# Layer norms taken row by row between the products of a macaron encoder layer

## The chip, the core and the metric

The kernel runs on one core of a Trainium2 chip. The time is the device time of one execution in microseconds (us). The core has five engines, each with its own queue of instructions that it works off in order: TensorE (PE) multiplies matrices, VectorE (DVE) and ScalarE (ACT) do arithmetic on rows, GpSimd (POOL) does some of it too and issues a few transfers, and SyncE (SP) issues nearly all transfers (DMAs) between device memory and the on-chip memory SBUF. Engines wait for each other by semaphores.

## The reference

One encoder layer, run on two inputs, of 512 and 1024 rows of 1024 values, with the same weights:

```
x = layer_norm(ALPHA * x + 0.5 * swiglu(x, ffn1_wg, ffn1_wu, ffn1_wd), ln_g[0], ln_b[0])
x = layer_norm(ALPHA * x + hybrid_mixer(x, ...),                       ln_g[1], ln_b[1])
x = layer_norm(ALPHA * x + 0.5 * swiglu(x, ffn2_wg, ffn2_wu, ffn2_wd), ln_g[2], ln_b[2])

def swiglu(x, wg, wu, wd):            # wg, wu: 1024 x 2816, wd: 2816 x 1024
    return (silu(x @ wg) * (x @ wu)) @ wd

def layer_norm(x, g, b):
    mu = mean(x); xc = x - mu; var = mean(xc * xc)
    return xc * rsqrt(var + 1e-5) * g + b
```

The mixer projects the rows to a gated recurrence, an attention and a Fourier part and joins them by an output projection. All is float32.

## The kernel before

The 1536 rows of both inputs form 12 tiles of 128 rows, a "row" from here on. `ffn` is called twice, as ffn1 ahead of the mixer and as ffn2 behind it. Each call handles the 12 rows in two halves of six: an early phase (`ffn1a`, half 0) and a late phase (`ffn1b`, half 1). A phase goes over 11 pairs (`NP`) of 256 hidden columns. Each pair has 14 "up" products, seven for each of the two blocks of hidden columns, because the matrices are multiplied by a scheme with seven products in the place of eight; a product is 12 matmuls of 128x384 (`up<-xt,…`). Every number is held as the sum of two fp32r pieces, a high and a low one: `split` makes them by a cast on ACT (L132) and a difference on DVE (L133), and `mm3` (L138) multiplies pieces three ways. From the products DVE and ACT form the hidden values `h`, and the "down" products of a pair (`big<-a,h`, `big<-w,h`) run between the up products of the next; DVE adds them to the six accumulators in SBUF (tile `x`, L456 and L509). In the early phase the prepared weights are written to device memory (`left`), and in the late phase `kept` reads them again (`w<-left`), two loads of 1 MB ahead, each for two products; only pair 0 of the late phase makes its pieces anew (`up<-xt,a`).

The layer norm of half 0 does not stand at the end of the early phase. It is a generator, `norm`, which is advanced from within the products of pair 0 of the late phase (by `between`), in two batches of three rows, by `layer_norm` (L210 to L240). A batch goes through these steps for its rows together: a mean on DVE (L222), a Square with a running sum on ACT (L225), the variance on DVE (L227), its power -0.5 on POOL (L228), and for each row a centre step on DVE (L231: subtract the mean, multiply by the gain). The final step scales by the power and adds the bias. For rows of odd number this is one DVE operation (L238). For rows of even number (`POOLED`) it is an Identity on ACT (L235) and an add on POOL (L236). Then SP stores each row (L240), and afterwards the next six rows are loaded into the freed slots (L160).

The norm of half 1 is at the end of the late phase: the accumulators are finished by the last down products (`down`, L447 to L456) in the row order `last` = 3, 0, 1, 2, 4, 5, and each row's norm follows as a batch of one. For ffn1 this overlaps with the entrance of the mixer: `columns` transposes rows of x1 on PE (`big<-ident,x`, L153), which come from device memory by `load_rows` (L160), and `project` multiplies them by the input weights (`big<-xt,w`). For ffn2 it is the end of the program.

The order on each engine is made by a scheduler from the order in which the code issues work and from priorities; within one engine nothing overtakes afterwards. Tiles live in pools of a few slots by name (`x` has six, `a` five), and an instruction that writes a tile waits until its slot is free.

Of the kernel before, what the change touches and what calls it, by code (L numbers as in the profile page):

```python
# [65 lines left out]
STAGE = 2  # L66
PREP = 3
STREAM = 2
DOWN_AT = (0, 1, 3, 4, 6, 8, 9, 11)
SCRATCH = 2048  # L70
SQ_SCALE = 2.0 ** 64
# [31 lines left out]
class Kernel:  # L103
# [106 lines left out]
    def layer_norm(self, rows, sums, params, dst=None, part=range(TPC)):  # L210

        nc = self.nc
        for t0 in part[::BATCH]:
            ts = range(t0, min(t0 + BATCH, part.stop))
            n = len(ts)
            st = self.tiny("st", [3, TPC])[:, :, :n]
            mean, var, rs = (st[:, i] for i in range(3))
            if sums.shape[2] > 1:
                nc.vector.tensor_reduce(mean, sums[:, t0:t0 + n], axis=mybir.AxisListType.X, op=ALU.add)
                nc.vector.tensor_scalar(mean, mean, -1.0 / D, None, op0=ALU.mult)  # L220
            else:
                nc.vector.tensor_scalar(mean, sums[:, t0:t0 + n, 0], -1.0 / D, None, op0=ALU.mult)  # L222
            for t in ts:
                k = t - t0
                nc.scalar.activation(self.slot("a", [D], BF16), rows[t], AF.Square, bias=mean[:, k:k + 1],  # L225
                                     accum_out=var[:, k:k + 1])
            nc.vector.tensor_scalar(var, var, 1.0 / D, EPS / ALPHA ** 2, op0=ALU.mult, op1=ALU.add)  # L227
            nc.gpsimd.tensor_tensor(rs, var, self.mhalf[:, :n], op=ALU.pow)  # L228
            for t in ts:
                a, k = rows[t], t - t0  # L230
                nc.vector.scalar_tensor_tensor(a, a, mean[:, k:k + 1], params[0], op0=ALU.add, op1=ALU.mult)  # L231
            for t in ts:
                a, k = rows[t], t - t0
                if POOLED(t):
                    nc.scalar.activation(a, a, AF.Identity, scale=rs[:, k:k + 1])  # L235
                    nc.gpsimd.tensor_add(a, a, params[1])  # L236
                else:
                    nc.vector.scalar_tensor_tensor(a, a, rs[:, k:k + 1], params[1], op0=ALU.mult, op1=ALU.add)  # L238
                if dst is not None:
                    STORE(nc, t).dma_start(dst[t], a)  # L240

# [79 lines left out]
    def ffn(self, n, which, src, dst, scr, wscr, first=False, beside=iter(()), staged=iter(()), meanwhile=iter(())):  # L321
# [72 lines left out]
        def up(m, w, got, between, result, fifth=quarter):  # L394
# [33 lines left out]
            out(m, got, 1, 0, a, result)  # L428
            yield

        def out(m, got, i, j, x, result):

            if m == 0:
# [75 lines left out]
                    nc.vector.scalar_tensor_tensor(x, ps, scale, x, op0=ALU.mult, op1=ALU.add)  # L509
                yield  # L510

        def norm(half, accs, parts):
            params = self.ln_params(which, "p")
            for part in parts:
                self.layer_norm(accs, sums[:, half] if half else sums[:, half, :, :1], params, dst[half * HALF:(half + 1) * HALF], part)
                yield

        def prepared(todo, keep):

# [12 lines left out]
        def kept(todo):  # L532
# [3 lines left out]
            def ahead(n=STREAM):  # L536
                while todo and len(slots) < n:
                    w = self.slot("w", [2, 2, h, P], F32R)
                    nc.sync.dma_start(f32(w), f32(todo.pop(0)))
                    slots.append(w)  # L540

            def get():
# [21 lines left out]
            raws = load(0)  # L564
            operand = self.operands_from(scr[0])
        both = lambda w, got, result: chain.from_iterable(zip(*(up(m, w, got, between, result) for m in range(2))))
        last = (3, 0, 1, 2, 4, 5)

        half, tiles = 0, []
        staging = self.operands_to(self.pairs(src[HALF:]), scr[1], [(k, r) for r in range(3) for k in SEVEN])  # L570
# [33 lines left out]
            run(tile() for tile in tiles)  # L604

        half, staging = 1, staged
        norms = norm(0, accs, [range(0, 3), range(3, 6)])
        get, ahead = kept([wscr[p][:, c:c + 2] for p in range(1, NP) for c in range(0, 2 * len(SEVEN), 2)])

        def between():  # L610
            if p == 0:
                next(norms, None)
            if STAGE <= p:
                next(staging, None)

        with self.phase(f"ffn{n}b", LATE_SLOTS, LATE_BANKS):
            steps = iter(())
            for p in range(NP):
                got = {}
                result = "a" if p == NP - 1 else None  # L620
                if p:
                    fifth = lambda: self.slot("d", [HT])
                    products = chain(*(up(m, get, got, between, result, fifth) for m in range(2)))
                else:
                    products = both(first_pair(raws, [[self.slot(t, [h, P]) for t in "bd"] for _ in raws]), got, result)
                for i, _ in enumerate(products):
                    if i in DOWN_AT:
                        next(steps, None)
                    if i == 8:
                        if p < NP - 1:  # L630
                            raw = load_both(p)
# [10 lines left out]
                    steps = down_seven(got, raw)  # L642
            run(staging)
            run(beside)
            norms = norm(1, accs, [range(t, t + 1) for t in last])
            for t in last:
                next(meanwhile, None)
                down(got, ws, t, True)
                next(norms)
            run(meanwhile)  # L650


    def project(self, xts):
# [488 lines left out]
    def run(self):  # L1142
        tc, nc, ins = self.tc, self.nc, self.ins
        with ExitStack() as ctx:
# [153 lines left out]
```

## Time and profile before

| | |
|---|---|
| median of 3 runs | 2902.63 us (2901.74 to 2905.0) |
| the profiled execution's own time | 2902.0 us |
| its span (first to last instruction) | 2899.9 us |
| mean granted TensorE clock | 0.976 of full speed |
| busy share of the span | PE 95%, DVE 67%, ACT 40%, POOL 5% |
| instructions | 39216 |

The busy shares are means over the whole span; what an edit touches is read from the stretch in which it lies. Timelines give the start of a run of like instructions, its length, and in brackets how long the engine had been idle ahead of it and who ended that. Matmuls are pipelined, so a busy PE is not PE at its peak; a lower granted clock shows as longer matmuls.

### The profile page before, as it was taken

Reading aid. Unit: us, or ns where it says so; the run is one execution under the profiler, and the core shown is the slowest. Engines: PE = TensorE matmul, PEld = TensorE weight load, DVE = VectorE, ACT = ScalarE, POOL = GpSimd, SP = SyncE. Lnnn points to the kernel's source line nnn. Section 1 sums busy time; section 2 is a strip of 40 time slices with the busy share of each in tenths; the row PEclk is TensorE's granted clock in tenths of the full one; section 3 lists DMA queues with packets and bytes.
Section 4 is the critical chain, followed back from the end, with each engine's and each line's share of the span. In section 5 each row is a group of like instructions: output and inputs, shape, how many; then the busy total and the mean of one; then the engine's idle time right before and its main releaser. Section 6 shows DMA issues by size and latency. Waiting matters only on the chain. (4 is left out here: it accounts for less than half of the span.)

```text
span 2899.9 us, 39216 instructions
## 1 busy us (share of the span) xinstructions
PE 2762.1 (95%) x14940; PEld 2521.3 (87%) x14940; DVE 1929.5 (67%) x3217; ACT 1157.9 (40%) x2093; POOL 135.1 (5%) x106
## 2 busy tenths in 40 slices
PE   8999999899999989999889986899999998999997
PEld 7999999799999978978678976799999998999996
DVE  7677666677676672453477754667766667676776
ACT  5344334333332344662365642344443334323223
POOL 2000000100000020000000011100000001000002
PEclk9999999999999999999899998899999999999999
DMA  7799766878555572244585486988876586555552
GB/s 255 267 317 317 281 239 227 302 282 271 198 183 193 183 241 83 96 159 141 171 235 153 136 277 216 339 291 303 296 280 242 211 310 221 201 187 191 190 186 104
DMA packets 318076, 650.48 MB, mean 224 GB/s; under 512 B 22976, under 2 KB 194624, under 8 KB 297408
## 3 DMA queue, kind: packets, MB, share of 16 engines
q1 hardware_dynamic: 313888, 641.16, 64.0%
q0 software_dynamic: 4000, 6.82, 0.9%
q8 instruction: 117, 1.92, 0.3%
q14 instruction: 71, 0.58, 0.1%
HBM read 403.06 MB, written 244.84 MB: 223 GB/s over the span
## 5 line engine op out<-in xcount | busy, mean ns | idle before, releaser
L138 PE MATMUL up<-xt,a 128*128 128x384 f32 x4032 | 746.8, 340 | 36.9 <-ACT a L132 27.3
L138 PEld LDWEIGHTS up<-xt,a 128*128 128x128 f32 x4032 | 710.8, 190 | 52.5 <-ACT a L132 31.8
L138 PE MATMUL up<-xt,w 128*128 128x384 f32 x3360 | 617.9, 337 | 0.0
L138 PEld LDWEIGHTS up<-xt,w 128*128 128x128 f32 x3360 | 588.6, 188 | 22.3 <-ACT t L422 10.0
L138 PE MATMUL big<-w,h 128*128 128x512 f32 x1584 | 387.1, 393 | 0.5 <-ACT h L132 0.2
L509 DVE SCALAR_TENSOR_TENSOR x<-big,x 128x512 f32<-128x512 f32 x420 | 277.7, 685 | 111.7 <-PE big L138 109.0
L138 PEld LDWEIGHTS big<-w,h 128*128 128x128 f32 x1584 | 295.3, 188 | 58.7 <-ACT h L132 1.6
L138 PE MATMUL big<-a,h 128*128 128x512 f32 x1260 | 317.9, 394 | 0.0
L138 PEld LDWEIGHTS big<-a,h 128*128 128x128 f32 x1260 | 234.0, 188 | 40.7
L138 PE MATMUL big<-xt,w 128*128 128x512 f32 x1008 | 234.3, 392 | 0.0
L456 DVE SCALAR_TENSOR_TENSOR x<-big,x 128x1024 f32<-128x1024 f32 (+1 forms) x156 | 177.2, 1138 | 81.0 <-PE big L138 78.5
L138 PEld LDWEIGHTS big<-xt,w 128*128 128x128 f32 x1008 | 189.7, 189 | 40.2 <-ACT x L961 0.4
L133 DVE TENSOR_TENSOR a<-w,a 128x512 fp32r<-128x512 f32 x244 | 166.2, 698 | 50.2 <-ACT a L132 48.4
L132 ACT CAST a<-w 128x512 fp32r<-128x512 f32 x244 | 147.6, 621 | 22.3 <-DMA w<-in_ffn_wg 14.0
L132 ACT CAST a<-b 128x512 fp32r<-128x512 f32 x168 | 103.8, 620 | 122.0 <-PE up L138 50.5
L133 DVE TENSOR_TENSOR a<-b,a 128x512 fp32r<-128x512 f32 x168 | 114.9, 688 | 42.9 <-ACT a L132 40.5
L132 ACT CAST h<-t 128x384 fp32r<-128x384 f32 x168 | 86.2, 513 | 119.5 <-DVE t L439 72.3
L138 PE MATMUL mm<-w,xt 128*128 128x256 f32 x960 | 122.4, 285 | 1.3 <-DVE x L1136 1.3
L138 PEld LDWEIGHTS mm<-w,xt 128*128 128x128 f32 x960 | 118.2, 193 | 2.0 <-DVE x L1136 1.9
L403 DVE TENSOR_TENSOR t<-t,up 128x384 f32<-128x384 f32 x88 | 48.7, 553 | 91.7 <-ACT t L402 91.3
L422 ACT COPY t<-up 128x384 f32<-128x384 f32 x88 | 42.2, 479 | 166.6 <-PE up L138 166.4
L414 ACT COPY t<-up 128x384 f32<-128x384 f32 x88 | 42.2, 479 | 161.8 <-PE up L138 161.8
(309 smaller groups left out, 3129.8 us busy)
## 6 DMA issues: line engine op xcount, KB each, us to landing
left<-a SPq DMA_DIRECT2D x280, 512.0 KB, 4.2
w<-left SPq DMA_DIRECT2D x140, 1024.0 KB, 4.7
ops<-a SPq DMA_DIRECT2D x63, 512.0 KB, 4.2
x<-x SPq DMA_DIRECT2D x52, 512.0 KB, 4.3
w<-in_ffn_wg SPq DMA_DIRECT2D x24, 1024.0 KB, 5.8
w<-in_ffn_wu SPq DMA_DIRECT2D x24, 1024.0 KB, 7.4
d<-in_ffn_wd SPq DMA_DIRECT2D x88, 256.0 KB, 4.5
w<-in_ffn_wd SPq DMA_DIRECT2D x20, 1024.0 KB, 5.0
```

The source lines that it names most:

```text
L132: self.nc.scalar.copy(hi, src)
L133: self.nc.vector.tensor_sub(lo, src, f32(hi))
L138: self.nc.tensor.matmul(out, lhs(l), rhs(r), start=first and n == 0, stop=last and n == 2, skip_group_check=onto)
L403: nc.vector.tensor_add(s, s, b)
L414: nc.scalar.copy(s, a)
L422: nc.scalar.copy(s2 := quarter(), a)
L456: nc.vector.scalar_tensor_tensor(accs[t][:, at], pd, scale, accs[t][:, at], op0=ALU.mult, op1=ALU.add, **acc)
L509: nc.vector.scalar_tensor_tensor(x, ps, scale, x, op0=ALU.mult, op1=ALU.add)
```

## The change

A new `layer_norm_row` handles one row: mean, Square, variance and power as before, the centre step on DVE, and the final step always on DVE; the Identity on ACT and the add on POOL are gone. It is a generator with three stages, and `norm` interleaves the stages of neighbouring rows. In pair 0 of the late phase it is advanced once behind each product. The order of rows is now 3, 4, 5, 0, 1, 2 at both places.

In the last pair the second block of products runs in another order (`up_late`, 1 2 3 4 5 0 6), so that the part of the hidden values that rows 3 to 5 need is complete one product before the end; `ending` starts the last down products and the norms after product 12. The weight loads of that pair, whose products are no longer neighbours in `left`, are split in two loads of 512 KB where needed.

Last, `ffn` returns its accumulators, and the mixer's columns for the second and third chunk of four rows are made from the rows in SBUF. Only rows 4 and 5 (half 0) are still loaded from device memory, into slots named `a`. Before, all eight were loaded into slots named `x`.

```diff
+LATE_ORDER = (1, 2, 3, 4, 5, 0, 6)
+    def layer_norm_row(self, a, sums, params, dst):
+        st = self.tiny("st", [3, TPC])
+        mean, var, rs = (st[:, i, :1] for i in range(3))
+        if sums.shape[1] > 1:
+            nc.vector.tensor_reduce(mean, sums, axis=mybir.AxisListType.X, op=ALU.add)
+            sums = mean
+        nc.vector.tensor_scalar(mean, sums, -1.0 / D, None, op0=ALU.mult)
+        nc.scalar.activation(self.slot("a", [D], BF16), a, AF.Square, bias=mean, accum_out=var)
+        yield
+        nc.vector.tensor_scalar(var, var, 1.0 / D, EPS / ALPHA ** 2, op0=ALU.mult, op1=ALU.add)
+        nc.gpsimd.tensor_tensor(rs, var, self.mhalf[:, :1], op=ALU.pow)
+        nc.vector.scalar_tensor_tensor(a, a, mean, params[0], op0=ALU.add, op1=ALU.mult)
+        yield
+        nc.vector.scalar_tensor_tensor(a, a, rs, params[1], op0=ALU.mult, op1=ALU.add)
+        nc.sync.dma_start(dst, a)
+        yield
...
-        def norm(half, accs, parts):
+        def norm(half, accs, rows):
             params = self.ln_params(which, "p")
-            for part in parts:
-                self.layer_norm(accs, sums[:, half] if half else sums[:, half, :, :1], params, dst[half * HALF:(half + 1) * HALF], part)
-                yield
+            late = iter(())
+            for t in rows:
+                row = self.layer_norm_row(accs[t], sums[:, half, t, :2 if half else 1], params, dst[half * HALF + t])
+                next(row)
+                next(late, None)
+                yield
+                next(row)
+                late = row
+                yield
+            next(late, None)
+            yield
...
-                    nc.sync.dma_start(f32(w), f32(todo.pop(0)))
+                    src, (x, y) = todo.pop(0)
+                    if y == x + 1:
+                        nc.sync.dma_start(f32(w), f32(src[:, x:y + 1]))
+                    else:
+                        for i, at in enumerate((x, y)):
+                            nc.sync.dma_start(f32(w)[:, i], f32(src[:, at]))
...
-        last = (3, 0, 1, 2, 4, 5)
+        last = (3, 4, 5, 0, 1, 2)
-        norms = norm(0, accs, [range(0, 3), range(3, 6)])
+        norms = norm(0, accs, last)
...
         def between():
-            if p == 0:
-                next(norms, None)
             if STAGE <= p:
                 next(staging, None)
+        def ending(got, ws):
+            norms = norm(1, accs, last)
+            for t in last:
+                down(got, ws, t, True)
+                next(norms)
+                next(norms)
+                next(meanwhile, None)
+                yield
+            run(norms)
...
-                    products = chain(*(up(m, get, got, between, result, fifth) for m in range(2)))
+                    forms = (up, up) if p < NP - 1 else (up, up_late)
+                    products = chain(*(form(m, get, got, between, result, fifth) for m, form in enumerate(forms)))
                 for i, _ in enumerate(products):
+                    if p == 0:
+                        next(norms, None)
                     if i in DOWN_AT:
                         next(steps, None)
+                    if p == NP - 1 and i == 12:
+                        run(steps)
+                        rest = ending(got, ws)
+                        next(rest)
...
-            xts = [self.columns_from(cols)] + [self.columns(lambda c=c: self.load_rows(chunk(x1, c), "x")) for c in range(1, NCH)]
+            held = []
+            xts = [self.columns_from(cols), self.columns(lambda: self.load_rows(x1[TPC:HALF], "a") + held[:2 * TPC - HALF]),
+                   self.columns(lambda: held[2 * TPC - HALF:])]
...
-            self.ffn(1, 0, xs, x1, scr[0], wscr, True, tables(), self.columns_to(chunk(x1, 0), cols), begun())
+            held += self.ffn(1, 0, xs, x1, scr[0], wscr, True, tables(), self.columns_to(chunk(x1, 0), cols), begun())
```

ACT in pair 0 of ffn1's late phase, before. L225 is the norm's Square, L235 its Identity for even rows, L132 the casts of weight pieces (`a<-b`, `a<-d`), and L402 to L414 copies of products.

```order
L225 ACTIVATE a,st<-x,st 128x1024 x2
L409 COPY t<-up 128x384
L225 ACTIVATE a,st<-x,st 128x1024
L132 CAST a<-b 128x512
L235 ACTIVATE x<-x,st 128x1024 x2
L409 COPY t<-up 128x384
L225 ACTIVATE a,st<-x,st 128x1024 x3
L132 CAST a<-b 128x512
L235 ACTIVATE x<-x,st 128x1024
L414 COPY t<-up 128x384
```

The same place after; L252 is the Square, L133 the casts, L422 and L429 the copies.

```order
L252 ACTIVATE a,st<-x,st 128x1024
L133 CAST a<-b 128x512
L133 CAST a<-d 128x512
L422 COPY t<-up 128x384
L252 ACTIVATE a,st<-x,st 128x1024
L489 ACTIVATE t<-t 128x384
L133 CAST a<-d 128x512
L422 COPY t<-up 128x384
L133 CAST a<-b 128x512
L429 COPY t<-up 128x384
L252 ACTIVATE a,st<-x,st 128x1024
```

The Squares of a batch stood together, and the Identities behind them; now one Square stands every three or four operations, and no Identity.

DVE in the same stretch, before: L227 is the variance, L231 the centre step, L238 the final step, L133 the low pieces (`a<-b,a`).

```order
L231 SCALAR_TENSOR_TENSOR x<-x,st,p 128x1024 x2
L227 TENSOR_SCALAR st<-st 128x3
L231 SCALAR_TENSOR_TENSOR x<-x,st,p 128x1024
L238 SCALAR_TENSOR_TENSOR x<-x,st,p 128x1024
L133 TENSOR_TENSOR a<-b,a 128x512
L231 SCALAR_TENSOR_TENSOR x<-x,st,p 128x1024 x2
L227 TENSOR_SCALAR st<-st 128x3
L231 SCALAR_TENSOR_TENSOR x<-x,st,p 128x1024
L238 SCALAR_TENSOR_TENSOR x<-x,st,p 128x1024 x2
```

After: L254 variance, L256 centre step, L258 final step, L134 the low pieces, L396 and L423 sums of weights and of products.

```order
L254 TENSOR_SCALAR st<-st 128x1
L256 SCALAR_TENSOR_TENSOR x<-x,st,p 128x1024
L134 TENSOR_TENSOR a<-b,a 128x512
L134 TENSOR_TENSOR a<-d,a 128x512
L258 SCALAR_TENSOR_TENSOR x<-x,st,p 128x1024
L423 TENSOR_TENSOR t<-t,up 128x384
L396 TENSOR_TENSOR b<-w,d 128x512
L254 TENSOR_SCALAR st<-st 128x1
L256 SCALAR_TENSOR_TENSOR x<-x,st,p 128x1024
L423 TENSOR_TENSOR t<-t,up 128x384
L134 TENSOR_TENSOR a<-d,a 128x512
```

Nine passes over whole rows stood with one low piece between them; now two to four other operations stand between one row's centre and final step, and there are twelve passes in all.

SP at the end of ffn1, before: L240 stores rows of x1 (`x_9` is row 3 of the late half, `x_6` its row 0), L160 loads rows of x1 for the mixer's columns, L144 and L792 load weights.

```order
L240 DMA x_9_129<-x 128x1024
L144 DMA a<-in_w_in 128x8x128
L160 DMA x<-x_4_124 128x1024
L144 DMA a<-in_w_in 128x8x128
L240 DMA x_6_126<-x 128x1024
L160 DMA x<-x_5_125 128x1024
L240 DMA x_7_127<-x 128x1024
L144 DMA r<-in_w_in 128x8x128
L240 DMA x_8_128<-x 128x1024
L160 DMA x<-x_6_126 128x1024
L240 DMA x_10_130<-x 128x1024
```

After, from the third of the stores on: L259 stores rows, L161 loads them, L145 loads weights, L762 stores columns of the mixer.

```order
L259 DMA x_11_131<-x 128x1024
L145 DMA a<-in_w_in 128x8x128
L145 DMA r<-in_w_in 128x8x128
L259 DMA x_6_126<-x 128x1024
L145 DMA r<-in_w_in 128x8x128
L259 DMA x_7_127<-x 128x1024
L762 DMA rx_76<-d 128x512
L161 DMA a<-x_4_124 128x1024
L161 DMA a<-x_5_125 128x1024
L259 DMA x_8_128<-x 128x1024
```

The loads of `x_4` and `x_5` stood behind one and two of the stores, and now stand behind five; the loads of the six other rows are gone.

## Rows read from the trace of the kernel before

**Rows 1.** Stretches: length, busy PE, PEld, DVE, ACT, POOL, granted clock, DMA.

```profile
546.76:589.12 42.36, 33.33 (x170) 31.39 (x168) 33.99 (x43) 22.65 (x40) 13.43 (x7) 0.84 0.66 248
1062.50:1076.14 13.64, 5.65 (x34) 5.05 (x33) 13.02 (x12) 7.12 (x9) 7.95 (x4) 0.75 0.73 240
2867.81:2899.90 32.09, 15.85 (x70) 12.77 (x69) 25.19 (x54) 11.09 (x16) 15.68 (x9) 0.78 0.25 98
```

**Rows 2.** Waits of PE, whole run: total us, times, longest us.

```profile
PE up L138 <- ACT a L132: 27.3, 8, 6.2
```

**Rows 3.** Timeline of PE, ffn1: start us, us, operation, [idle before, releaser].

```profile
546.76 19.07 PE L138 MATMUL up<-xt,a 128*128 128x384 f32 x108
568.40 1.01 PE L138 MATMUL up<-xt,a 128*128 128x384 f32 x2 [2.57 <-ACT a L132]
574.53 1.91 PE L138 MATMUL up<-xt,a 128*128 128x384 f32 x4 [5.12 <-ACT a L132]
577.78 11.50 PE L138 MATMUL up<-xt,a 128*128 128x384 f32 x54 [1.34 <-DVE a L133]
589.12 6.92 PE L138 MATMUL up<-xt,w 128*128 128x384 f32 x39
...
599.54 1.78 PE L138 MATMUL big<-a,h 128*128 128x512 f32 x7
```

**Rows 4.** Timeline of ACT, the same stretch of ffn1.

```profile
561.88 2.19 ACT L235 ACTIVATE x<-x,st 128x1024 f32<-128x1024 f32 x2 [1.66 <-POOL st L228]
...
572.45 1.15 ACT L235 ACTIVATE x<-x,st 128x1024 f32<-128x1024 f32 x1 [4.09 <-POOL st L228]
```

**Rows 5.** Timeline of DVE, the same stretch of ffn1.

```profile
565.61 4.79 DVE L231 SCALAR_TENSOR_TENSOR x<-x,st,p 128x1024 f32<-128x1024 f32 x2 [1.84 <-ACT a L225]
570.32 0.15 DVE L227 TENSOR_SCALAR st<-st 128x3 f32<-128x3 f32 x1
...
572.45 4.67 DVE L238 SCALAR_TENSOR_TENSOR x<-x,st,p 128x1024 f32<-128x1024 f32 x2 [0.78 <-POOL st L228]
...
577.65 1.28 DVE L133 TENSOR_TENSOR a<-d,a 128x512 fp32r<-128x512 f32 x2
```

**Rows 6.** Timeline of POOL, the same stretch of ffn1.

```profile
563.12 6.19 POOL L236 TENSOR_TENSOR x<-x,p 128x1024 f32<-128x1024 f32 x2 [1.27 <-ACT x L235]
```

**Rows 7.** Timeline of PE, the same place in ffn2.

```profile
2382.91 19.05 PE L138 MATMUL up<-xt,a 128*128 128x384 f32 x108
...
2435.77 1.55 PE L138 MATMUL big<-a,h 128*128 128x512 f32 x6
```

**Rows 8.** Timeline of PE, end of ffn1 and entrance of the mixer.

```profile
1062.74 1.03 PE L153 MATMUL big<-ident,x 128*128 128x128 f32 x8
1070.07 3.56 PE L153 MATMUL big<-ident,x 128*128 128x128 f32 x16 [6.29 <-ACT d L678]
1075.32 1.07 PE L153 MATMUL big<-ident,x 128*128 128x128 f32 x8 [1.70 <-DMA x<-x]
```

**Rows 9.** Timeline of DVE, and of POOL at 2883.22, end of the program.

```profile
2882.01 2.33 DVE L231 SCALAR_TENSOR_TENSOR x<-x,st,p 128x1024 f32<-128x1024 f32 x1
...
2883.22 2.79 POOL L228 TENSOR_TENSOR st<-st,mhalf 128x1 f32<-128x1 f32 x2
...
2884.34 1.27 DVE L231 SCALAR_TENSOR_TENSOR x<-x,st,p 128x1024 f32<-128x1024 f32 x1
...
2888.98 1.73 DVE L231 SCALAR_TENSOR_TENSOR x<-x,st,p 128x1024 f32<-128x1024 f32 x1
...
2892.40 3.39 DVE L238 SCALAR_TENSOR_TENSOR x<-x,st,p 128x1024 f32<-128x1024 f32 x1 [0.44 <-POOL st L228]
```

**Rows 10.** Timeline of SP's queue, ffn1.

```profile
585.62 1.51 SPq L539 DMA_DIRECT2D w<-left  x2
```

**Rows 11.** DMA issues, whole run: count, KB each, median us to landing.

```profile
w<-left SPq DMA_DIRECT2D x140, 1024.0 KB, 4.7
x<-x SPq DMA_DIRECT2D x52, 512.0 KB, 4.3
```

More of the change, by code (lines that the diff above doesn't have):

```diff
@@ L240, in layer_norm @@
                     STORE(nc, t).dma_start(dst[t], a)
+    def layer_norm_row(self, a, sums, params, dst):
+        nc = self.nc
+        st = self.tiny("st", [3, TPC])
[13 more added lines that the diff above has]
+        yield
     def seven(self, rows, store, order, add):
@@ L429, in up, with up_late @@
             yield
+        def up_late(m, w, got, between, result, fifth):
+            a = self.psum("up", [CH])[:, :HT]
+            product(a, w(), 1)
+            s = quarter()
+            nc.scalar.copy(s, a)
+            yield
+            c = self.psum("up", [CH])[:, :HT]
+            product(c, w(), 2)
+            p5 = fifth()
+            nc.scalar.copy(p5, c)
+            yield
+            product(a, w(), 3, True)
+            s1 = quarter()
+            nc.scalar.copy(s1, a)
+            yield
+            product(c, w(), 4, True)
+            nc.vector.tensor_add(s1, s1, c)
+            out(m, got, 0, 1, s1, result)
+            yield
+            product(a, w(), 5, True)
+            nc.scalar.copy(s2 := quarter(), a)
+            nc.vector.tensor_add(s2, s2, p5)
+            out(m, got, 1, 1, s2, result)
+            yield
+            b = self.psum("up", [CH])[:, :HT]
+            product(b, w(), 0)
+            nc.vector.tensor_add(s, s, b)
+            out(m, got, 0, 0, s, result)
+            yield
+            product(a, w(), 6, True)
+            out(m, got, 1, 0, a, result)
+            yield
         def out(m, got, i, j, x, result):
@@ L510, in down_seven @@
                 yield
-        def norm(half, accs, parts):
+        def norm(half, accs, rows):
             params = self.ln_params(which, "p")
-            for part in parts:
-                self.layer_norm(accs, sums[:, half] if half else sums[:, half, :, :1], params, dst[half * HALF:(half + 1) * HALF], part)
-                yield
+            late = iter(())
[3 more added lines that the diff above has]
+                next(late, None)
+                yield
+                next(row)
+                late = row
+                yield
+            next(late, None)
+            yield
         def prepared(todo, keep):
@@ L606, in ffn @@
         half, staging = 1, staged
-        norms = norm(0, accs, [range(0, 3), range(3, 6)])
-        get, ahead = kept([wscr[p][:, c:c + 2] for p in range(1, NP) for c in range(0, 2 * len(SEVEN), 2)])
+        norms = norm(0, accs, last)
+        order = [m * len(SEVEN) + k for m in range(2) for k in SEVEN]
+        late = order[:len(SEVEN)] + [len(SEVEN) + k for k in LATE_ORDER]
+        get, ahead = kept([(wscr[p], o[c:c + 2]) for p in range(1, NP) for o in (order if p < NP - 1 else late,)
+                           for c in range(0, len(o), 2)])
         def between():
-            if p == 0:
-                next(norms, None)
             if STAGE <= p:
                 next(staging, None)
+        def ending(got, ws):
[5 more added lines that the diff above has]
+                next(meanwhile, None)
+                yield
+            run(norms)
         with self.phase(f"ffn{n}b", LATE_SLOTS, LATE_BANKS):
@@ L644, in ffn @@
             run(beside)
[L645 to L649, printed above, removed]
+            run(rest)
             run(meanwhile)
+        return accs
     def project(self, xts):
```

## The prediction

> **What bounds the kernel now.** First the busy times by stretch, to see where TensorE (PE) is not the bound. It fills most of the span; the stretches that the change touches are the exceptions [rows 1]. In the 42.36 us from the first product of the late half's pair 0 in ffn1 (call that moment T, 546.76) to the first product of pair 1, PE has 33.33 us of work at a mean granted clock of 0.84. Next the waits of PE: the largest single releaser is the cast of weight pieces on ScalarE (ACT), 27.3 us in 8 waits [rows 2]. Then PE's timeline from T [rows 3]. 108 matmuls of 128x384 run in 19.07 us, 0.177 us each; then three holes of 2.57, 5.12 and 1.34 us, and the 54 matmuls behind them take 11.50 us, 0.213 each, at the lowered clock. All 168 at 0.177 would be 29.7 us, so 42.36 - 29.7 = 12.6 us are lost, 9.0 idle and 3.6 clock. ffn2 has the same figures to 0.1 us [rows 7].
>
> Why PE waits is on the other engines' timelines. ACT has two Identity operations of the norm (L235) at 561.88, behind a power on POOL, and a third at 572.45 after 4.09 us in which it waited for POOL [rows 4]; queued behind it are a copy and the casts of the next weight pieces. VectorE (DVE) runs two centre steps at 565.61 in 4.79 us and two finals at 572.45 in 4.67 [rows 5], where one alone takes 1.27 [rows 9], because POOL adds beside them, 6.19 us for two [rows 6]. So it is a queue problem: the products stand behind a batched norm that goes through three engines.
>
> **Pair 0 of the late half, ffn1.** The change drops both batches (L235, L236) and has each row's two DVE passes spread over the 14 products. DVE gains three finals, 3 x 1.20 (1.27 less the 0.07 by which two operations overlap) = 3.6 us, and 9 small operations of 0.07 to 0.15 [rows 5], about 1.0. It loses what POOL's adds cost it: 4.79 + 4.67 - 4 x 1.20 = 4.7. So DVE's work stays as it is, about 34 of the 42.36 us [rows 1], and nobody on ACT waits for a power any more. By that DVE cannot do the old stretch in much under 34 us, while PE needs 29.7: DVE becomes nearly the bound.
>
> I walked the new order with these durations, each engine in its own order. DVE waits about 2 us for the first Square, then keeps each weight piece 1.6 to 2.8 us ahead of its product, so the products end at T + 29.8. PE goes on with 48 matmuls of pair 1 (39 before), 8.5 us, to T + 38.3, and meets the first h piece, which DVE reaches after the last norm row (T + 33) and some ten splits and sums of 0.6 to 0.7 [rows 5], at T + 39.5. The second block of down products then ends its wait at T + 43.4; before it began at 599.54 [rows 3], T + 52.8. That is 9.4 us.
>
> One more queue is moved past: SP. Loads of pair 1's weights (w from left) stand behind the row stores, and behind the loads of new rows into the slots that the stores set free. The first such weight load was issued at 585.62 [rows 10]. Now: the last final at T + 33 (579.8), its store lands 4.3 later (the row load's median, for want of the store's own), the load into its slot is issued, then the weights at about 585, landing 4.7 later [rows 11] at 589.7 to 591. They are wanted at T + 43.4 = 590.2. So 0 to 1.5 us are lost there; I take 1.4. Sum for ffn1: **8**, from 3 (if DVE runs at 0.3 us more per product, 14 x 0.3 = 4.2, and the load as much later) to 12.6.
>
> **The same place in ffn2.** The lost time is the same, and the second down block began at 2435.77, T + 52.9 [rows 7]. Here DVE's new order has the h splits directly after the last norm row; the walk puts the first block at T + 34 and the second at T + 40.6. That would be 12.3. Three row loads behind the last store may be up to 1 us late, so **11**, from 4 to 12.6.
>
> **End of ffn1 into the mixer.** After ffn1's last down products PE transposes rows of x1 and waits 6.29 us for an ACT copy that stands behind L235 again, and 1.70 for a row load [rows 8]; with the lowered clock (0.75 in 13.6 us, [rows 1]) about 10 us are lost. The change feeds the mixer from SBUF rows, so six of eight row loads of 4.3 us [rows 11] vanish, and rows 3 to 5 finish first. But the two loads that remain, of rows 4 and 5, now stand on SP behind the stores of five late rows, each of which waits for its final on DVE; before the first stood behind one. In the walk it is issued 32 us after row 3's first down product, lands at 36.5, PE being free at 29.8, and the next projection block starts at about 41 instead of 44.2. That is **3**, from -2 (each us by which the finals of the late rows slip goes straight into it) to 6.
>
> **End of the program.** From the last product on, 32.09 us pass, of which PE needs 15.85 and DVE 25.19 [rows 1]: DVE bounds it. DVE gains three finals, 3.6 us, and loses the contention with POOL's adds, (2.33 - 1.27) + (1.73 - 1.27) + (3.39 - 1.27) = 3.6 [rows 9]. The chain of the last row (square, variance, power beside centre, final, store) is the same. So **0**, from -3 to +3 (longer). The new order of last products moves one product by one place and adds nothing to PE; the weight loads split in two are 512 KB each and are far ahead of use, 0.
>
> Sum: 8 + 11 + 3 + 0 = 22 us off 2902.0, the profiled execution's own time (span 2899.9); the median of the runs is 0.6 above it. Forecast **2880**.
>
> **A rule that speaks against it.** While POOL runs its powers, DVE's centre step of 1.27 us at 2884.34 lies inside the 2.79 us of powers from 2883.22 on [rows 9], and is not slowed. POOL's adds do slow it. The Trainium skill, SBUF — State Buffer, section Who interferes with whom, says that a DVE instruction with two SBUF inputs contends with a GpSimd instruction that reads SBUF, and that the one which comes second blocks until the first is done. By that rule, the power would hold the centre step that the new order puts right beside it in each of the 24 rows. The adds bear the rule out, the power on one column does not.
>
> **The rivals.**
> - DVE is the bound. DVE's work of 34 us stands in a stretch in which the products themselves ask for 29.7, and the walk leaves DVE nearly no idle time; in the old run it idled some 11 us between T and the first h. If ordinary gaps of 0.3 us per product remain, ffn1 gives 3 to 5, ffn2 6 to 8, the mixer 1, the tail 0: about 12, **2890**. For it: the balance above. Against it: the pieces run 1.6 to 2.8 us ahead.
> - All of it comes: 12.6 + 12.6 + 6 - 3 (tail) = 28, **2874**. It needs DVE to be free whenever PE asks, which its share speaks against.
> - It does nothing: the holes only move from the casts to pair 1's weight loads behind the stores on SP, or to its h pieces. Then pair 1's down block stays near T + 50 in both ffns, and the time is **2900**.
> - Slower: the power holds DVE. Place: the centre step beside the power of each row. Price: up to 1.4 us (2.79 for two, [rows 9]) in each of 24 rows. In the two pair 0 stretches 6 x 1.4 = 8.4 us eat the gain of 8 and most of the 11; in the mixer's entrance 8.4 turn +3 into -5; at the program's end DVE is the bound and 8.4 go straight onto the end. Sum 0 + 3 - 5 - 8 = -10: **2912**. It decides from about 1 us per row on; at 2884.34 it was nothing.
>
> **How the numbers follow.** The forecast (2873 to 2886) has 0.50, DVE as the bound (2886 to 2896) 0.25, all of it (below 2873) 0.06, nothing (2897 to 2908) 0.11, slower by the power or late stores 0.08. The range for 8 in 10 runs from 2871 to 2897: it holds the forecast, the DVE bound and part of the best case. A measurement of this kernel can tell about 0.2%, 5.8 us, from no change: faster than 2896.8 has 0.81, within 0.11, slower 0.08.
>
> **What would show it.** In the new profile: PE's holes of 2.57, 5.12 and 1.34 gone, and the 168 matmuls of pair 0 in 30 to 32 us at a clock near 1.0; no Identity of the norm on ACT and no add on POOL there; DVE's centre steps at 1.27 with no 2.3 us ones (if they take 2 us or more beside a power, the rule above was right); the second down block of pair 1 at T + 43 to 45 in ffn1 and T + 41 to 42 in ffn2; the weight load behind the last row store landing no later than T + 45; the first projection block after the transposes about 41 us after row 3's down product; the stretch from last product to end still 32 us. The forecast is wrong if PE waits for DVE's splits within pair 0 by more than 4 us, if the row loads into the mixer come more than 40 us after row 3's first down product, or if the tail is over 35.

## The result and the profile after

| | before | after |
|---|---|---|
| median of the runs | 2902.18 us (2901.71 to 2905.0) | 2882.18 us (2879.53 to 2886.49) |
| ratio, 95% interval | | 0.993, 0.9913 to 0.9948 |
| the profiled execution's own time | 2902.0 us | 2879.53 us |
| span, mean granted clock | 2899.9 us, 0.976 | 2877.6 us, 0.98 |

The forecast was 2880 in a range from 2871 to 2897. The time falls by 20 us in the medians and by 22.3 us between the spans of the two profiled executions. To see where, the span is cut at five starts of matmul groups on PE's timeline that both kernels have: T1 and T2 (the first product of the late phase's pair 0 in ffn1 and ffn2), P1 and P2 (the first down product of row 3 in the last pair of each, `big<-w,a`) and M (the projection block behind the mixer's first transposes).

| stretch | before, us | after, us | measured | predicted |
|---|---|---|---|---|
| start to T1 | 546.8 | 547.8 | +1.0 | 0 |
| T1 to P1 | 485.2 | 475.9 | -9.3 | -8 |
| P1 to M | 44.2 | 44.7 | +0.5 | -3 |
| M to T2 | 1306.8 | 1305.6 | -1.2 | 0 |
| T2 to P2 | 482.0 | 469.1 | -12.8 | -11 |
| P2 to the end | 35.0 | 34.5 | -0.6 | 0 |
| span | 2899.9 | 2877.6 | -22.3 | -22 |

The gain is in the two late phases. PE's timeline of the changed kernel in ffn1, where [rows 3] had three holes (start us, length us, operation, count, in brackets the idle time ahead and who ended it):

```profile
547.80 29.31 PE L139 MATMUL up<-xt,a 128*128 128x384 f32 x168
576.95 8.49 PE L139 MATMUL up<-xt,w 128*128 128x384 f32 x48
586.97 2.35 PE L139 MATMUL big<-a,h 128*128 128x512 f32 x9 [1.53 <-ACT h L133]
591.15 2.35 PE L139 MATMUL big<-a,h 128*128 128x512 f32 x9 [1.83 <-ACT h L133]
```

All 168 matmuls of pair 0 run without a break, at 0.174 us each. The second down block begins 43.35 us after T1, where before it was 52.8. What is left are 3.4 us in which PE waits for `h` pieces. In ffn2 only 0.25 us of this is left; from T2 = 2373.99 to the second down block at 2414.07 it is 40.1 us, before 52.9 [rows 7]:

```profile
2403.13 4.33 PE L139 MATMUL up<-xt,w 128*128 128x384 f32 x24
2407.29 0.62 PE L139 MATMUL big<-a,h 128*128 128x512 f32 x2
2408.16 1.88 PE L139 MATMUL big<-a,h 128*128 128x512 f32 x7 [0.25 <-DVE h L134]
2409.88 4.35 PE L139 MATMUL up<-xt,w 128*128 128x384 f32 x24
2414.07 2.24 PE L139 MATMUL big<-a,h 128*128 128x512 f32 x9
```

The busy times by stretch (length; PE, PEld, DVE, ACT, POOL busy; granted clock, DMA share, GB/s) say it once more, beside [rows 1]. The granted clock is 1.00 where it was 0.84:

```profile
547.80:576.95 29.15, 29.15 (x170) 29.14 (x168) 25.92 (x43) 17.91 (x34) 12.01 (x7) 1.00 0.79 289
2373.99:2403.13 29.14, 29.14 (x169) 29.14 (x168) 25.93 (x43) 17.92 (x34) 10.84 (x5) 1.00 0.82 299
1053.00:1068.37 15.37, 6.58 (x33) 6.37 (x33) 11.17 (x11) 6.21 (x8) 5.00 (x2) 0.67 0.88 287
```

The third row is the mixer's entrance, where PE works 6.6 of 15.4 us. There PE's timeline shows the wait for the two loads of rows 4 and 5:

```profile
1062.00 3.67 PE L154 MATMUL big<-ident,a 128*128 128x128 f32 x16 [8.79 <-DMA a<-x]
1065.47 3.15 PE L154 MATMUL big<-ident,x 128*128 128x128 f32 x16
1068.37 16.63 PE L139 MATMUL big<-xt,w 128*128 128x512 f32 x72
```

SP's timeline shows when they were issued, behind the fifth store of a row:

```profile
1054.87 0.34 SPq L259 DMA_DIRECT2D x<-x  x1
1055.50 0.34 SPq L762 DMA_DIRECT2D rx<-d  x1
1055.88 1.85 SPq L161 DMA_DIRECT2D a<-x  x2
```

In [rows 8] the same place had 6.29 us behind an ACT copy and 1.70 behind a row load, 8.0 us together; now it is 8.8 us behind one of the two.

### The profile page after: what moved, and what is told of

Its sections match the earlier page's. It is cut to its first block, busy times and chain, and to the rows that moved or that the text cites. A ratio compares the mean times of both kernels' runs of the same rounds, so it can differ in the third digit from the quotient of the medians.

```text
span 2877.6 us, 39226 instructions
## 1 busy us (share of the span) xinstructions
PE 2757.0 (96%) x14940; PEld 2520.7 (88%) x14940; DVE 1928.2 (67%) x3245; ACT 1145.8 (40%) x2081; POOL 121.3 (4%) x102
## 5 line engine op out<-in xcount | busy, mean ns | idle before, releaser
L139 PE MATMUL up<-xt,a 128*128 128x384 f32 x4032 | 739.8, 339 | 18.7 <-ACT a L133 12.3
L139 PEld LDWEIGHTS big<-a,h 128*128 128x128 f32 x1260 | 233.9, 188 | 45.3 <-ACT h L133 4.1
L134 DVE TENSOR_TENSOR a<-w,a 128x512 fp32r<-128x512 f32 x244 | 166.4, 700 | 50.0 <-ACT a L133 49.7
L133 ACT CAST a<-w 128x512 fp32r<-128x512 f32 x244 | 147.7, 621 | 25.9 <-DMA w<-in_ffn_wg 13.0
L133 ACT CAST a<-b 128x512 fp32r<-128x512 f32 x168 | 103.9, 621 | 97.4 <-PE up L139 36.9
L134 DVE TENSOR_TENSOR a<-b,a 128x512 fp32r<-128x512 f32 x168 | 115.0, 689 | 40.7 <-ACT a L133 38.4
L133 ACT CAST h<-t 128x384 fp32r<-128x384 f32 x168 | 86.1, 513 | 120.8 <-DVE t L493 74.2
L255 POOL TENSOR_TENSOR st<-st,mhalf 128x1 f32<-128x1 f32 x24 | 44.0, 1833 | 1455.5 <-DVE st L254 1455.5
L423 DVE TENSOR_TENSOR t<-t,up 128x384 f32<-128x384 f32 x86 | 47.6, 553 | 86.0 <-ACT t L422 85.7
L434 ACT COPY t<-up 128x384 f32<-128x384 f32 x86 | 41.3, 480 | 158.3 <-PE up L139 158.3
```

The source lines that it names most:

```text
L133: self.nc.scalar.copy(hi, src)
L134: self.nc.vector.tensor_sub(lo, src, f32(hi))
L139: self.nc.tensor.matmul(out, lhs(l), rhs(r), start=first and n == 0, stop=last and n == 2, skip_group_check=onto)
L255: nc.gpsimd.tensor_tensor(rs, var, self.mhalf[:, :1], op=ALU.pow)
L423: nc.vector.tensor_add(s, s, b)
L434: nc.scalar.copy(s, a)
```

## The experiments

The theory (A): the whole gain comes from pair 0 of the late phases, where the norm's batches through ACT and POOL made PE's holes. Rivals: the last pair's order and the mixer's rows carry a part of it (B); the batching as such made the holes, not the route of the final step (A2); DVE is the bound now (E). Three kernels take back one part of the change each, others cut one cause, and two try what the traces suggest. Totals of one kernel scatter by some us, so the stretches of the table above are compared, and the totals as ratios to the kernel before on the same chip.

| kernel | median us | ratio to before (95%) | T1-P1 | P1-M | T2-P2 | P2-end |
|---|---|---|---|---|---|---|
| before | | | 485.2 | 44.2 | 482.0 | 35.0 |
| changed | 2882.18 | 0.993 (0.9913 to 0.9948) | 475.9 | 44.7 | 469.1 | 34.5 |
| changed, again | 2881.40 | 0.992 (0.9902 to 0.9937) | 478.9 | 44.8 | 469.3 | 34.5 |
| batch0 | 2902.00 | 0.9996 (0.9987 to 1.0005) | 485.3 | 45.4 | 482.2 | 34.5 |
| order_back | 2883.83 | 0.9934 (0.9919 to 0.9949) | 478.7 | 47.5 | 469.2 | 35.1 |
| cols_dram | 2882.29 | 0.9928 (0.9914 to 0.9943) | 476.1 | 42.6 | 469.2 | 34.6 |
| pooled | 2895.22 | 0.9969 (0.996 to 0.9979) | 485.6 | 44.8 | 474.8 | 35.0 |
| act_dve | 2882.49 | 0.9928 (0.9911 to 0.9946) | 474.9 | 45.3 | 469.6 | 34.5 |
| dve_more | 2878.14 | 0.9909 (0.9894 to 0.9924) | 473.4 | 44.2 | 470.7 | 34.5 |
| hoist | 2879.19 | 0.9915 (0.9899 to 0.9931) | 476.2 | 43.4 | 469.3 | 34.5 |
| tables_later | 2879.59 | 0.9919 (0.9903 to 0.9935) | 472.7 | 45.3 | 469.2 | 34.5 |
| one_mean | 2879.92 | 0.9919 (0.9904 to 0.9934) | 476.2 | 44.2 | 469.2 | 33.2 |
| best | 2875.01 | 0.9898 (0.9882 to 0.9914) | 472.9 | 43.0 | 469.4 | 33.0 |
| best_dram | 2874.27 | 0.9899 (0.9884 to 0.9914) | 472.8 | 43.2 | 469.3 | 33.2 |

**The changed kernel once more.** No edit.

> The changed kernel itself once more, beside its variants on one chip. All theories: 0.993 of the kernel before, as measured, so some 20 us under it; in the profile the second down block of pair 1 43.4 us behind the first product of pair 0 in ffn1 and 39.4 in ffn2, and 44.7 us from row 3's first down product to the next projection block.

Measured: 0.992. Its span was 2887.0 us, 9.4 more than in the first profile, of which 6.7 lie between M and T2 (1312.3 against 1305.6), in a stretch that the change does not touch, and 3.0 in T1 to P1. T2-P2 and P2-end repeat to 0.2 us and P1-M to 0.1. So a difference of 3 us in T1-P1 alone is within what two runs of one kernel show. P1-M lies between 44.2 and 45.4 in the kernels below whose edits touch neither the last pair's order nor the mixer's rows, so about 1 us there says little. The 39.4 us expected for ffn2 were counted from a matmul 0.7 us behind T2; from T2 on it is 40.1 in both profiles, and the gain of 13.5 us named for ffn2 in the next expectation is 12.8.

**Batches back in half 0.** `norm` calls the old batched function for half 0, from `between`:

```diff
+            if half == 0:
+                for part in (range(0, 3), range(3, 6)):
+                    self.layer_norm(accs, sums[:, half, :, :1], params, dst[:HALF], part)
+                    yield
+                return
```

> Only the norm of half 0 (pair 0 of the late phase) is put back to two batches of three rows with the old operations; the last pair, the norm of half 1 and the mixer's rows stay as changed. Theory A (the whole gain lies in pair 0, 9.4 us in ffn1 and 13.5 in ffn2 by the two traces): 22 us slower than the changed kernel, 2900 to 2906, with the holes of 2.6, 5.1 and 1.3 us back. Rival B (the last pair's order and the mixer's rows carry a share): under 2895.

Measured: 2902.0, a ratio of 0.9996, with the last pair's new order and the mixer's SBUF rows still in. On PE's timeline the holes are back, to 0.1 us:

```profile
546.89 19.07 PE L139 MATMUL up<-xt,a 128*128 128x384 f32 x108
568.53 0.91 PE L139 MATMUL up<-xt,a 128*128 128x384 f32 x2 [2.57 <-ACT a L133]
574.66 1.91 PE L139 MATMUL up<-xt,a 128*128 128x384 f32 x4 [5.22 <-ACT a L133]
577.91 11.64 PE L139 MATMUL up<-xt,a 128*128 128x384 f32 x54 [1.34 <-DVE a L134]
```

Theory A holds, and B falls: everything else in the change, taken together, is worth nothing that can be measured. Its parts earn and cost 2 to 3 us each, as the next two kernels show.

**The last pair's order back.** `last = (3, 0, 1, 2, 4, 5)` in half 1, `up` in the place of `up_late`, and `ending` behind the last product.

> The last pair has its old product order and the rows of half 1 their old order 3 0 1 2 4 5, the last down products start behind the last product; half 0's norm row by row and the mixer's rows as changed. Theory A: within 3 us of the changed kernel, since the end of the program came out only 0.6 us shorter. Rival B: the earlier finish of rows 3 to 5 earns 4 us or more at either end, so 2887 to 2892.

Measured: 0.9934, within the scatter of the changed kernel. In the stretches the new order does earn 2.8 us at the mixer's entrance (47.5 against 44.7) and 0.6 at the end of the program.

**The mixer's rows from device memory.** The line that builds `xts` is the old one again, with eight loads into `x` slots.

> The mixer's columns of chunks 1 and 2 are loaded from device memory again, eight loads into x slots; all else as changed. The prediction's step (SBUF rows earn 3 us at the mixer's entrance): 3 to 6 us slower than the changed kernel. Rival C (the remaining load of rows 4 and 5 behind five row stores gives that away, as the trace with 44.7 us from row 3's first down product to the next projection block against 44.2 before lets one think): within 2 us, or even faster by 2.

Measured: 0.9928, and the entrance is 2.1 us shorter than in the changed kernel (42.6 against 44.7). So the SBUF rows do not earn the predicted 3 us, they cost 2 there. What differs is on SP's timeline of this kernel. The first two row loads are issued at 1044.19, behind the third store of a row, and not at 1055.88 as above:

```profile
1043.12 0.54 SPq L259 DMA_DIRECT2D x<-x  x1
1043.75 0.39 SPq L145 DMA_DIRECT2D a<-in_w_in  x1
1044.19 1.54 SPq L161 DMA_DIRECT2D x<-x  x2
```

**The two loads earlier.** `ending` issues them behind row 3's down products:

```diff
                 next(norms)
+                if t == last[0] and early is not None:
+                    early()
                 next(norms)
...
+                             lambda: kept_rows.extend(self.load_rows(x1[TPC:HALF], "a")))
```

> Only the two loads of rows 4 and 5 for the mixer are issued earlier, ahead of the stores of half 1's rows. Theory C (the prediction's 3 us at the mixer's entrance are missing because these loads stand behind five row stores): the 8.8 us for which PE waits for them go, the next projection block starts 36 to 38 us after row 3's first down product, the kernel is 6 to 9 us faster than the changed one. Rival D (something else is late next: the input weights, whose loads now find two slots fewer, or ACT's copies): under 3 us faster.

Measured: 0.9915, P1-M 43.4, a gain of 1.3 us where theory C had 6 to 9, and little more than the scatter of this stretch. Rival D is right. PE's wait for the load is gone, and behind it stands another nearly as long, for an ACT copy out of PSUM (the memory into which PE writes):

```profile
1054.41 1.03 PE L154 MATMUL big<-ident,a 128*128 128x128 f32 x8
1062.59 1.97 PE L154 MATMUL big<-ident,a 128*128 128x128 f32 x8 [7.15 <-ACT d L763]
```

ACT's timeline ahead of that copy (L763 at 1061.96) has a Square that waited for a row's mean on DVE and a cast that waited for a weight load, whose issue on SP stands behind three row stores:

```profile
1056.85 1.15 ACT L252 ACTIVATE a<-x,st 128x1024 bf16<-128x1024 f32 x1 [3.85 <-DVE st L251]
1057.91 0.19 ACT L252 ACTIVATION_READ_ACCUMULATOR a<-x,st 128x1 f32 x1
1061.01 1.04 ACT L133 CAST w<-r 128x1024 fp32r<-128x1024 f32 x1 [2.91 <-DMA r<-in_w_in]
1061.96 0.58 ACT L763 COPY d<-big 128x512 f32<-128x512 f32 x1
```

The entrance has two ways that end within some 2 us of each other, and both lead back to DVE, which has 35.0 us of work in the 39.8 from the end of the last product to M in the changed kernel.

**Even rows by ACT and POOL, but row by row.** In half 0 only:

```diff
-        nc.vector.scalar_tensor_tensor(a, a, rs, params[1], op0=ALU.mult, op1=ALU.add)
+        if pooled:
+            nc.scalar.activation(a, a, AF.Identity, scale=rs)
+            nc.gpsimd.tensor_add(a, a, params[1])
+        else:
+            nc.vector.scalar_tensor_tensor(a, a, rs, params[1], op0=ALU.mult, op1=ALU.add)
```

> Row by row and spread over the products as changed, but in half 0 the even rows' final step goes by an Identity on ACT and an add on POOL again. Theory A1 (the chain over three engines makes the holes: ACT stands behind POOL's power, and POOL's adds slow DVE): 8 to 18 us slower than the changed kernel, 2890 to 2900. Rival A2 (the batching made them; a single row's power of 1.5 us is over when ACT comes to it): within 4 us, 2880 to 2886.

Measured: 0.9969, 2895.2; some 13 us are lost again, as A1 had it and not A2. But 7 us of the gain stay, all of them in ffn2: T2-P2 is 474.8 (482.2 with the batches, 469.1 as changed), while in ffn1 nothing is left (485.6, with the batches 485.3). So in ffn2 the batching did carry a part. Batches with the final step on DVE were not run; what batching costs without POOL's adds stays open. **The same with the add on DVE** parts what A1 had put together (`nc.vector.tensor_add` in the place of `nc.gpsimd.tensor_add`):

> As the variant with Identity on ACT and add on POOL for half 0's even rows, but the add on DVE: ACT still has the Identity behind the power, POOL adds nothing. If ACT's wait for the power made the 13 us of that variant: 8 us or more slower than the changed kernel. If POOL's adds did, by slowing DVE: within 4 us of the changed kernel, though DVE has three more passes per batch.

Measured: 0.9928, no slower than the changed kernel, in either late phase. So, taken row by row, ACT's Identity behind the power does no harm by itself; POOL's adds do. Three things are seen in the kernel with POOL's adds. First, its adds and some DVE passes do not run side by side but one behind the other. On POOL's timeline an add takes 3.92 us:

```profile
557.95 3.92 POOL L260 TENSOR_TENSOR x<-x,p 128x1024 f32<-128x1024 f32 x1 [1.27 <-ACT x L259]
```

On DVE's, two sums (L403) end at 559.61, 2.3 us ahead of the add's end, and the centre step that follows takes 3.36 and ends 1.1 us behind the add:

```profile
558.32 1.29 DVE L403 TENSOR_TENSOR d<-w 128x512 f32<-128x512 f32 x2
559.59 3.36 DVE L256 SCALAR_TENSOR_TENSOR x<-x,st,p 128x1024 f32<-128x1024 f32 x1
```

Second, ACT waits 7.8 us for powers in that stretch (1.9 with the add on DVE). The two powers that make most of it stand behind no add; they are slow themselves, beside DVE's passes. The last takes 4.20 us (2.06 with the add on DVE):

```profile
575.99 4.20 POOL L255 TENSOR_TENSOR st<-st,mhalf 128x1 f32<-128x1 f32 x1 [2.54 <-DVE st L254]
```

Third, the last row's store comes late. On SP's timeline it is issued at 583.88 (579.95 in the changed kernel), and behind it stand row loads and the stores of the mixer's tables:

```profile
583.88 0.33 SPq L263 DMA_DIRECT2D x<-x  x1
584.26 2.92 SPq L161 DMA_DIRECT2D x<-in_x_sample  x3
587.27 0.86 SPq L1274 DMA_DIRECT2D dft<-b  x2
```

A table's store sets free a `b` slot, and DVE's timeline shows its wait for that slot, ahead of the first `h`:

```profile
594.05 0.56 DVE L529 TENSOR_TENSOR b<-t 128x384 f32<-128x384 f32 x1 [7.15 <-DMA dft<-b]
```

**More work on DVE.** One more pass over each row of half 0 between centre and final step, a sum that nobody reads:

```diff
+                if half == 0:
+                    nc.vector.tensor_reduce(sums[:, 0, t, 1:], accs[t], axis=mybir.AxisListType.X, op=ALU.add)
```

> In pair 0 of each late phase DVE has one more pass over each row (a sum over 1024 columns that nobody reads, about 1.1 us, 6.6 per phase), between centre and final step. Theory E (DVE is now the bound of that stretch, as its 35 to 39 us of work in 39 to 43 us say): the second down blocks come 5 to 6.6 us later in both ffns, 10 to 13 us slower than the changed kernel. Rival F (DVE has slack there): under 4 us slower.

Measured: 0.9909, not slower at all; T1-P1 is 2.5 us shorter, T2-P2 1.6 longer. E falls, with a limit. The scheduler answered the longer DVE work with another order. On PE's timeline products of pair 1 now run among those of pair 0,

```profile
546.51 25.59 PE L139 MATMUL up<-xt,a 128*128 128x384 f32 x146
571.93 0.33 PE L139 MATMUL up<-xt,w 128*128 128x384 f32 x1
572.11 1.89 PE L139 MATMUL up<-xt,a 128*128 128x384 f32 x10
573.84 0.68 PE L139 MATMUL up<-xt,w 128*128 128x384 f32 x3
```

and the table store is done when its slot is wanted. So 6.8 us more (six times 1.13) fit into the stretch in this order, in which PE has other products to take; what the unchanged order would have lost by it was not tried, and how much the earlier table stores give back is not parted from it.

**Tables later.** In the late phase, pair 0 leaves out its step of the table transfers (`if p == 0: … else: next(beside, None)`).

> Only the transfers of the mixer's tables no longer run in pair 0 of ffn1's late phase; all else as changed. Theory G (the 3.4 us that PE still waits there stand behind one of the two b slots which a table's store holds, and behind row loads): ffn1's stretch from the first product of pair 0 to row 3's first down product falls from 475.9 to about 473 us, ffn2's stays at 469.2. Rival H (DVE's own work is the bound there): it stays above 475.

Measured: T1-P1 472.7, and PE's idle time in the first 85 us from T1 falls from 3.4 to 0.24 us. In the changed kernel the wait is on DVE's timeline, ahead of the first `h`:

```profile
585.81 0.56 DVE L525 TENSOR_TENSOR b<-t 128x384 f32<-128x384 f32 x1 [0.60 <-DMA dft<-b]
```

The wait itself is 0.6 us (1.54 in its second profile, where T1-P1 was 3 us longer). The scheduler also uses the free slot to put the first down block behind 24 matmuls of pair 1 instead of 48. The two kernels below that hold this edit too have 472.8 and 472.9, against 475.9 to 478.9 in the six runs with pair 0 as changed, so the gain is more than scatter. Theory G holds for the place; how much is the wait and how much the order is not parted.

**One operation for the mean.** Half 1's rows, whose sum comes in two halves:

```diff
-            nc.vector.tensor_reduce(mean, sums, axis=mybir.AxisListType.X, op=ALU.add)
-            sums = mean
+            nc.vector.tensor_scalar(mean, sums[:, :1], sums[:, 1:], -1.0 / D, op0=ALU.add, op1=ALU.mult)
```

> Only the mean of half 1's rows in one DVE operation instead of two. From row 3's first down product to the end of the program 33.0 to 33.4 us instead of 34.5 (theory: at the end the last row's Square stands behind another row's final step and its wait for the power), nothing elsewhere. Rival: the scheduler's other order costs as much, 34 us or more.

Measured: P2 to the end 33.2 us, 1.3 less, nothing elsewhere. On DVE's timeline of the changed kernel the second step of the last row's mean (L251) stands behind another row's final step, and DVE then waits 1.39 us for that last row's Square:

```profile
2867.77 0.14 DVE L249 TENSOR_REDUCE st<-sums 128x1 f32<-128x2 f32 x1
2868.30 1.29 DVE L258 SCALAR_TENSOR_TENSOR x<-x,st,p 128x1024 f32<-128x1024 f32 x1 [0.38 <-POOL st L255]
2869.50 0.15 DVE L251 TENSOR_SCALAR st<-st 128x1 f32<-128x1 f32 x1
2871.03 0.15 DVE L254 TENSOR_SCALAR st<-st 128x1 f32<-128x1 f32 x1 [1.39 <-ACT a L252]
```

**Together.** The early loads, the one-operation mean and the later tables:

> The early loads of rows 4 and 5, and two more edits: the mean of half 1's rows in one DVE operation instead of two, so that the last row's Square no longer stands behind another row's final step (1.5 us at the end of the program by the trace), and no table transfers in pair 0 of the late phase, where DVE waited 0.6 us for one of their slots. Expected: the early loads' gain and 1 to 3 us more. Rival: the scheduler's other order costs as much, and it equals the kernel with the early loads alone.

and the last two of them with device loads in the mixer:

> The one-operation mean and the later tables, with the mixer's eight row loads from device memory as in the kernel before. If the loads of rows from SBUF earn nothing at the mixer's entrance (42.6 us with device loads, 44.7 as changed, 43.0 with the early loads, in the runs so far), this equals the kernel with all three edits or is up to 1 us faster; if they do, it is 2 us or more slower.

Measured: 0.9898 and 0.9899, 2875.0 and 2874.3. Both beat the kernel before by 28 us. Against the changed kernel on the same chip (0.992) the first gains 6.4 us of the medians, though the intervals still touch. They are equal to each other. Rows taken from SBUF earn nothing: with the two loads early they equal rows from device memory, with the loads late they cost 2 us at the entrance.

## Why the prediction was right, step by step

*The sum.* 22 us were forecast and 22.3 measured, but that they are so near is in part luck: the two late phases gave 3 us more than was taken for them, and the mixer's entrance 3.5 us less.

*What bounds the kernel.* Right: PE's 27.3 us behind ACT's casts [rows 2] are now 12.3, and the holes are gone.

*Pair 0 in ffn1.* Predicted 43.4 us from T1 to the second down block, measured 43.35; the products end at T1 + 29.2, predicted 29.8. The stretch gives 9.3 where 8 were taken. The 1.4 us taken off for SP were the step that failed: the four weight loads behind the last row store were issued from 583.82 on, 36.0 us after T1 where 38.2 were assumed, and PE did not wait for them (SP's timeline):

```profile
579.95 0.33 SPq L259 DMA_DIRECT2D x<-x  x1
...
583.82 2.77 SPq L604 DMA_DIRECT2D w<-left  x4
```

SP's queue did cost something, but by other entries in it: a table's store, which the prediction did not name (0.60 us of DVE's wait ahead of the first `h`), and the last row load, for which DVE waits ahead of a down product's sum:

```profile
588.20 0.69 DVE L563 SCALAR_TENSOR_TENSOR x<-big,x 128x512 f32<-128x512 f32 x1 [0.69 <-DMA x<-in_x_sample]
```

The walk's 43.4 held neither of these waits, so that it was met to 0.05 us is in part luck. That such an entry can be worth 7 us is seen when the last row store comes 4 us later, in the kernel with POOL's adds.

*ffn2.* 12.8 measured, 11 taken; the walk's 12.3 was the better number (down blocks at T2 + 33.3 and 40.1, walked 34 and 40.6), and the late row loads cost nothing.

*The cause.* The prediction held ACT's wait behind the power for the head of the chain and POOL's adds for a cost beside it. The two kernels with an Identity on ACT turn this round, as far as rows taken one by one go: with the add on DVE the wait costs nothing, with the add on POOL 13 us. In the kernel with POOL's adds DVE is slowed, two powers are slow, and the last store is late. In the batches ACT's wait was longer (1.66 and 4.09 us [rows 4]); what it cost there without POOL's adds is not shown. The balance of DVE's work (3.6 us for finals against 4.7 for contention) had this right in its sum.

*DVE as the next bound.* Mis-sized. DVE has 25.9 of 29.15 us of work there, and 6.8 us more do not slow the kernel in the order that the scheduler then makes, with other products on PE.

*The mixer's entrance.* This term was wrong, +0.5 in the place of -3. The walk had the load issued 32 us after P1 and it was (32.2); PE was free at 29.5 (29.8 predicted). But PE could start 6.1 us after the issue of the first load, where 4.3 were taken for its landing. That term was mis-sized on the trace of the kernel before: the line `x<-x` of [rows 11] puts 28 loads of rows and 24 stores of rows together, and apart their medians are 6.1 and 3.0 us. From PE's start to M it took 6.4 us for 32 transposes where the walk has 4.5; the granted clock over the wait and the transposes was 0.67. So M came at 44.7 and not at 41. And the term had only one wait in view. With the load early the ACT copy is late at nearly the same time, which the prediction did not walk.

*The end of the program.* Predicted 0, measured -0.6. DVE has its 3 finals more, POOL's adds are gone, and the two are equal, as the sum said: with the last pair's old order the stretch is 35.1 us, before it was 35.0. The 0.6 belong to the new order, which the prediction put at 0.

*The rule.* The 24 centre steps took 1.273 to 1.281 us, so the slower rival falls. In ffn1's late phase a power begins some 0.2 us behind each. The groups by line, DVE's first (shortest, median, longest in ns, then the first and the last start):

```profile
L256 DVE SCALAR_TENSOR_TENSOR x<-x,st,p x24: 1273/1275/1281, 551.5 to 2871.1; 128x1024 f32<-128x1024 f32 x24
```

and POOL's powers:

```profile
L255 POOL TENSOR_TENSOR st<-st,mhalf x24: 1283/1462/3517, 551.7 to 2871.3; 128x1 f32<-128x1 f32 x24
```

The power is second to come here, and some of the powers take 2 to 3.5 us. The Trainium skill, SBUF — State Buffer, section Who interferes with whom, says that the one which comes second waits until the first is done. The trace agrees, with POOL as the one that waits: each of the 24 powers ends 0.41 to 0.43 us behind the end of a DVE operation with two inputs in SBUF, the centre step or a later one. One of the slow powers, to 574.09, and the DVE operation that ends at 573.68:

```profile
571.10 2.99 POOL L255 TENSOR_TENSOR st<-st,mhalf 128x1 f32<-128x1 f32 x1 [2.59 <-DVE st L254]
573.13 0.55 DVE L443 TENSOR_TENSOR t<-t 128x384 f32<-128x384 f32 x1
```

So the prediction's reading that the power on one column does not bear the rule out was wrong. Its own rows show the same: the second of the two powers of [rows 9] ends at 2886.01, 0.40 us behind the centre step that ends at 2885.61. The prediction had read the rule as a charge on DVE and forgotten to ask which of the two issues first. DVE pays only where it stands waiting for a slow power, 0.4 to 0.5 us ahead of some final steps.

## What to carry to other kernels

When a step goes over three engines, ask for each leg what it does to the queue it leaves, not only what it costs: here 13 of 22 us hung on which engine did one add, while the wait that the profile named first cost nothing once the rows went one by one and the add had moved. A transfer is as late as the slowest thing ahead of it in its queue, so list what stands behind a store that waits for arithmetic (weight loads, slots of tables, rows for the next stage) and which slot each of them sets free. Where two waits end at about the same time, as at the mixer's entrance, taking one away gives the difference between them, 1.3 us of 8.8.

## What the hardware showed that was not expected

- A DVE pass over 1024 columns beside a POOL add over as many took 3.36 us and the add 3.92, where others of their kind took 1.27 and 2.4; beside a POOL power on one column the pass took 1.28 in all 24 cases, and the power ended 0.41 to 0.43 us behind it or behind a later DVE operation with two inputs in SBUF, up to 3.5 us after its own start.
- Loads and stores of rows of the same size, 512 KB, that one line of the list of issues puts together with a median of 4.3 us to landing, have medians of 6.1 and 3.0 us apart (28 and 24 of them, kernel before). The two loads at the mixer's entrance took 6.1 and 6.6, with the DMA engines busy to 0.88.
- Two profiles of the same kernel differ by 9.4 us of span, and 6.7 of that lie in a stretch in which nothing was changed.
